# Two-layer decoder trunk with routed experts: the residual's rows turned while the experts are chosen, the last expert in two pieces, and a branch hint

## The chip, the cores and the metric

The kernel runs on one core of a Trainium2 chip. The metric is the device time of one execution in microseconds (us); the time quoted for a kernel is the median of its runs. One execution more was taken with the hardware profiler; the profile's times count from the start of that execution's span. PE is TensorE, with PEld its weight loads; ACT is ScalarE, DVE is VectorE, POOL is GpSimd, and SP is the engine whose queue carries the weight transfers.

## What is computed

A trunk of two layers over 256 tokens of width 1024, in float32. Layer 0 mixes with retention, layer 1 with native sparse attention. After each mixing comes the same end, on which the change works (cut from the reference):

```python
def moe(h, router_w, router_b, w_gate, w_up, w_down):      # 16 experts of width 512
    aff = jax.nn.sigmoid((x @ router_w).astype(jnp.float32))
    ...                                                     # best group of 4, its top 2 experts
    for e in range(N_EXPERTS):
        he = (jax.nn.silu(x @ w_gate[e]) * (x @ w_up[e])) @ w_down[e]
        y = y + w[:, e:e + 1] * he

h = layer_norm(ALPHA * h + mix, ln_mix_g[l], ln_mix_b[l])
h = layer_norm(ALPHA * h + moe(h, ...), ln_ffn_g[l], ln_ffn_b[l])
```

So each layer needs, besides the experts' outputs, the residual ALPHA * h added to them, where h is the normalised row times a per-column scale plus a shift.

## The kernel before

The 256 tokens are two blocks of 128 rows (`tb`). Every weight streams once from HBM in chunks of 1 MB over SP's queue, through a ring of SBUF places; a chunk is asked for when the place that it takes is free. Products that need float32 accuracy on f32r data use a high and a low part (`hilo`: ACT casts the high part, DVE subtracts to get the low one). The weights of the dense layers are split so as well, 1024 columns at a time (L114 on ACT, L115 on DVE); the experts' weights are multiplied as plain f32, each such matmul standing in the trace as two records.

After the mixing, `mix_norm` ends the layer's first half. It copies the rows to SBUF as `r`, transposes `r` in f32 on PE to get the router's logits, normalises `r` in place (without scale and shift), and splits it into `hh` (ACT, L569) and `hl` (POOL, L577). Then PE has to wait for DVE, which ranks the experts; in that time it is kept at work by matmuls whose results nobody reads: `warm` (L252, 20 in layer 0 and 12 in layer 1, from the table `WARM`), and two f32 matmuls of 512 columns behind it (L625). `ACT` loads its Silu table there. `route` (L681 to L683, then the one-hot matrices L709) ends the choice.

`experts` gathers each expert's tokens into 64 slots by multiplying `hh` and `hl` with one-hot matrices (L727). ACT (L735) and DVE (L733) take the result out of PSUM and apply scale and shift on the way. For each expert e the loop then runs `gate_up` of expert e+1 (16 chunk halves, L776, 64 slots by 512 columns), `hidden` (Silu on ACT L795, product on DVE L796), and `down` of expert e (L776 on hT). In the middle of a `gate_up` PE does the `fill`: `turn` (transposes of the hidden rows, L804), `scatter` (the expert's output, split by `hilo` on ACT L222 and DVE L223, is added to the four PSUM banks `y` through the one-hot matrix, L825), parts of the next gather, and the residual: `alpha` (L832 to L846). In the fills of experts 0 to 7 `alpha` transposes one 128-column part of `hh` and of `hl` for both blocks (four transposes, L837), ACT and DVE scale, shift and add them into `al` (L839, L840), and the next fill adds `al` to `y` with the matrix ALPHA * identity (L844).

The last expert has no `gate_up` beside it. So PE runs, one behind the other: down(14), turn, scatter(14), down(15), and scatter(15), which waits for ACT and DVE to split the output of down(15). Then the row statistics of the final norm start on DVE (L306).

Each expert takes 64 tokens. Should one have more, `overflow` (L862 on) does the rest in a loop under `If(most > 64)`, L880, between hidden(14) and down(13). With these inputs no expert has more, so all engines jump over that body, some hundred PE instructions. In layer 0 the splitting of the next layer's dense weights begins during the last two experts (`split_ahead`): two halves of 1024 columns before down(14), two before down(15).

Of the kernel before, what the change touches and what calls it, by code (L numbers as in the profile page):

```python
# [10 lines left out]
F32 = mybir.dt.float32  # L11
# [18 lines left out]
WARM = 10, 20, 20, 12  # L30
# [123 lines left out]
class Trunk:  # L154
# [50 lines left out]

    def split_ahead(self, n):

        self.W.limit = 2 * self.moe_end(0) + n
        self.W.ahead()
# [314 lines left out]
    def mix_norm(self, keep, pool, y, tail, hh, low_parts, l, acc):  # L524
# [23 lines left out]

        def logits(tb, nh):
# [55 lines left out]
        turn(1, 1)  # L605
        end1 = dev(1)
# [4 lines left out]
        logits(1, 1)  # L611
        minus(1)
# [20 lines left out]
        return self.sums(acc, f"y_moe{l}"), oh, rest, hl  # L633
# [80 lines left out]
    def experts(self, pool, keep, oh0, rest, hh, hl, y, l):  # L714
        nc = self.nc
        iota = self.cst[:, C_IOTA:C_IOTA + 64]
# [90 lines left out]
        def down(e, hT):  # L807

            b = [self.bank(), self.bank()]
            for k in range(4):  # L810
                both(hT[:, k, :], self.W.get(2)[0], b, k == 0, k == 3)
            if not out:
                out.append(self.first.tile([P, 2048], F32R, tag="raw", name=f"out{l}"))
            d = []
            for i in range(2):
                t = out[0][:, i * 512:i * 512 + 512]
                hi, lo = t[64 * i:64 * i + 64], t[64 - 64 * i:128 - 64 * i]
                self.hilo(hi, lo, b[i][64 * i:64 * i + 64, :])
                d.append(t)
            return d  # L820

        def scatter(e, d, last):

            o = oT[e // 4][:, e % 2, e % 4 // 2]
            return [lambda tb=tb, nh=nh: nc.tensor.matmul(y[tb][nh], o[:, tb, :], d[nh], start=(e == 0), stop=last)  # L825
                    for nh in range(2) for tb in range(2)]

        def alpha():

            ts = {}  # L830

            def scaled(k):  # L832
                c = slice(k * P, k * P + P)
                b = self.bank()
                for i, x in enumerate((hh, hl)):
                    for tb in range(2):
                        nc.tensor.transpose(b[:, (2 * i + tb) * P:(2 * i + tb + 1) * P], x[tb][:, c].bitcast(F32), self.ident)  # L837
# [736 lines left out]
```

## Time and profile before

| what | value |
|---|---|
| median of 3 runs | 890.33 us (889.71 to 890.62) |
| profiled execution: its time, its span | 891.96 us, 890.1 us |
| mean granted TensorE clock, of full speed | 0.98 |
| PE, DVE, ACT, POOL busy in the span | 95%, 46%, 38%, 6% |
| HBM, mean over the span | 291 GB/s |
| experts of layer 0, first gather to the final statistics | 228.3 to 458.0 us |
| experts of layer 1 | 647.3 to 877.1 us |

A duration of an instruction in the rows below is the time from its start to its end; matmuls overlap, so the time that one of a row of matmuls takes from PE is the distance to the next one's start. The part in brackets behind a row is the time that the engine was idle before it, and what released it.

### The profile page before, as it was taken

What the parts mean: (1) busy time and instruction counts of PE and PEld (TensorE: products, weight loads), DVE (VectorE), ACT (ScalarE), POOL (GpSimd) and SP (SyncE); (2) the same over time, 40 slices, a digit from 0 to 9 for tenths busy, and PEclk for the clock granted to TensorE, in tenths of its full rate; (3) what the DMA queues carried; (4) which work ended last, traced back from release to release, by engine and by line L of the source; (5) the groups of instructions that cost most, each with busy time, mean ns of one, the idle gap of its engine ahead of it and who ended that gap; (6) DMA issues with size and microseconds to landing.
All of it is one profiled execution on the core that took longest, in us unless ns stands there. A gap on an engine that the chain in (4) does not pass through costs nothing. (4 is left out here: it accounts for less than half of the span.)

```text
span 890.1 us, 12109 instructions
## 1 busy us (share of the span) xinstructions
PE 846.9 (95%) x4738; PEld 535.0 (60%) x4738; DVE 405.6 (46%) x817; ACT 339.7 (38%) x657; POOL 50.0 (6%) x70
## 2 busy tenths in 40 slices
PE   7999999998999999999879998999999999999993
PEld 5998989886545454453338786666744545445431
DVE  4666776864422132221077877775433222222215
ACT  4335344434332331322164455785523233232312
POOL 1000000000200000000000004220110000000001
PEclk8999999999999999999999999899999999999997
DMA  9966354578699999999943456205779999999801
GB/s 332 426 248 231 119 218 142 190 279 350 224 409 410 426 423 427 422 425 423 365 156 138 169 230 237 96 1 203 308 280 388 425 427 424 427 426 427 375 3 47
DMA packets 37283, 259.83 MB, mean 292 GB/s; under 512 B 4217, under 2 KB 4401, under 8 KB 6369
## 3 DMA queue, kind: packets, MB, share of 16 engines
q1 hardware_dynamic: 36432, 255.87, 71.3%
q0 software_dynamic: 640, 2.97, 1.0%
q8 instruction: 42, 0.69, 0.3%
q14 instruction: 25, 0.20, 0.1%
q10 hardware_dynamic: 144, 0.11, 0.0%
HBM read 257.88 MB, written 1.05 MB: 291 GB/s over the span
## 5 line engine op out<-in xcount | busy, mean ns | idle before, releaser
L776 PE MATMUL bank<-raw,xT 128*64 128x512 f32 x1024 | 233.9, 596 | 0.8 <-ACT xT L735 0.8
L776 PEld LDWEIGHTS bank<-raw,xT 128*64 128x64 f32 x1024 | 76.7, 137 | 125.9 <-issue 118.5
L115 DVE TENSOR_TENSOR st<-raw,st 128x1024 fp32r<-128x1024 f32 x92 | 111.4, 1234 | 55.4 <-ACT st L114 55.3
L114 ACT CAST st<-raw 128x1024 fp32r<-128x1024 f32 x92 | 94.5, 1048 | 80.4 <-PE bank L339 32.4
L776 PE MATMUL bank<-raw,hT 128*64 128x512 f32 x512 | 118.6, 601 | 5.2 <-PEq L880 3.3
L323 PE MATMUL bank<-xh,st 128*128 128x256 f32 x512 | 93.6, 284 | 3.0 <-ACT st L114 2.5
L223 DVE TENSOR_TENSOR out<-bank,out 64x512 fp32r<-64x512 f32 x64 | 44.1, 689 | 96.7 <-ACT out L222 95.6
L776 PEld LDWEIGHTS bank<-raw,hT 128*64 128x64 f32 x512 | 40.5, 138 | 73.3 <-issue 70.1
L323 PEld LDWEIGHTS bank<-xh,st 128*128 128x128 f32 x512 | 80.4, 192 | 3.6 <-ACT st L114 2.7
L222 ACT CAST out<-bank 64x512 fp32r<-64x512 f32 x64 | 37.1, 579 | 104.6 <-PE bank L776 103.8
L323 PE MATMUL bank<-xl,st 128*128 128x256 f32 x256 | 72.3, 283 | 0.0
L796 DVE SCALAR_TENSOR_TENSOR sh<-bank,wsl,sh 64x512 f32<-64x512 f32 x32 | 23.7, 741 | 105.3 <-ACT sh L795 105.1
L795 ACT ACTIVATE sh<-bank 64x512 f32<-64x512 f32 x32 | 19.0, 593 | 94.9 <-PE bank L776 94.9
L323 PEld LDWEIGHTS bank<-xl,st 128*128 128x128 f32 x256 | 49.6, 194 | 0.1
L805 ACT COPY hT<-bank 128x256 f32<-128x256 f32 x32 | 11.9, 373 | 86.9 <-PE bank L804 86.9
L356 PE MATMUL acc<-st,gh 128*128 128x512 f32 x128 | 42.9, 407 | 1.8 <-DVE st L115 1.1
L339 PE MATMUL bank<-st,hTh 128*128 128x512 f32 x128 | 42.2, 401 | 1.7 <-DVE nt L1022 1.4
L825 PE MATMUL y_moe<-out 128*128 128x512 f32 x128 | 38.6, 419 | 4.4 <-DVE out L223 4.4
L840 DVE SCALAR_TENSOR_TENSOR al<-bank,wsm,al 128x256 f32<-128x256 f32 x16 | 7.7, 484 | 72.0 <-ACT al L839 72.0
L339 PE MATMUL bank<-st,xh 128*128 128x512 f32 x128 | 40.5, 393 | 0.0
L733 DVE TENSOR_SCALAR xT<-bank,wsm 128x128 f32<-128x128 f32 x64 | 21.9, 404 | 34.0 <-PE bank L727 24.2
L735 ACT ACTIVATE xT<-bank,wsm 128x128 f32<-128x128 f32 x64 | 24.1, 456 | 19.3 <-PE bank L727 19.3
(328 smaller groups left out, 1205.4 us busy)
## 6 DMA issues: line engine op xcount, KB each, us to landing
raw<-in_w_moe_dram SPq DMA_DIRECT2D x190, 1024.0 KB, 10.3
raw<-in_w_dense_dram SPq DMA_DIRECT2D x49, 1024.0 KB, 7.0
raw<-in_w_moe_dram SPq DMA_DIRECT2D x4, 512.0 KB, 15.6
xT<-in_x_T_dram SPq DMA_DIRECT2D x4, 256.0 KB, 5.4
raw<-in_w_dense_dram SPq DMA_DIRECT2D x2, 512.0 KB, 10.0
rt<-in_c_ret_dram POOLq DMA_DIRECT2D x1, 1024.0 KB, 11.1
gb<-in_ln_rows_dram POOLq DMA_DIRECT2D x1, 1024.0 KB, 6.9
out_dram<-lf_n SPq DMA_DIRECT2D x4, 256.0 KB, 2.0
```

The source lines that it names most:

```text
L114: self.nc.scalar.copy(hi, r)
L115: (eng or self.nc.vector).tensor_sub(lo, r, hi.bitcast(F32))
L222: self.nc.scalar.copy(hi, src)
L223: self.nc.vector.tensor_sub(lo, src, hi.bitcast(F32))
L323: self.nc.tensor.matmul(b[:, m, :], w[:, kk, c], x[:, k, :], start=(k == 0 and i == 0 and m == 0), stop=(k == 7 and i == 2 and m == 1))
L339: self.nc.tensor.matmul(b[tb], x[:, k, c], w[:, kk, :], start=(k == 0 and i == 0), stop=(k == 7 and i == 2))
L356: self.nc.tensor.matmul(y[tb][nh], x[a][:, c], w[b][:, 0, n], start=False, stop=last and i == 2)
L733: nc.vector.tensor_scalar(t, v, c, d, op0=ALU.mult, op1=ALU.add)
L735: nc.scalar.activation(t, v, AF.Identity, bias=d, scale=c)
L776: nc.tensor.matmul(b[i][c, :], x, w[:, i, :], start=first, stop=last)
L796: nc.vector.scalar_tensor_tensor(rows[0:64], b[0:64], w, rows[0:64], op0=ALU.mult, op1=ALU.mult)
L825: return [lambda tb=tb, nh=nh: nc.tensor.matmul(y[tb][nh], o[:, tb, :], d[nh], start=(e == 0), stop=last) for nh in range(2) for tb in ran ...
```

## The change

1. **Residual.** `mix_norm` transposes the normalised f32 rows `r` themselves, eight 128-column parts for each of the two blocks (`turned`): block 0 into two banks of the rotating PSUM pool, ahead of the warm-up, block 1 into two of the banks of `y`, behind the warm-up. In `experts`, ACT alone scales and shifts them into SBUF: block 0 ahead of the first gather's evacuations, block 1 behind the issue of gate_up(0). All adds to `y` come in two lots, in the fills of gate_up(0) and gate_up(1), and now open the accumulation.
2. **Warm-up.** `WARM` goes from 20 and 12 to 8 and 8, and the two f32 matmuls of L625 go. The load of ACT's Silu table moves behind the first gather.
3. **Branch.** The If's branch gets a hint "likely taken" for PE, placed at the start of the block in which the If stands.
4. **Dense weights.** In layer 0 three halves are split right behind the If, ahead of the splitting of down(13)'s output; the fourth follows later, in the final norm.
5. **Last expert.** The transposes for expert 15 stand in the middle of down(14); down(15) runs as two pieces of 256 columns, each with its own splitting by ACT and DVE; scatter(14) stands behind the second piece.

The core of the diff:

```diff
-WARM = 10, 20, 20, 12
+WARM = 10, 20, 8, 8
@@ mix_norm
+        def turned(tb, nh, b):
+            for k in range(4):
+                nc.tensor.transpose(b[:, k * P:k * P + P], half(r, tb, nh)[:, k * P:k * P + P], self.ident)
...
         turn(1, 1)
+        y_moe = self.sums(acc, f"y_moe{l}")
+        rows = [[self.bank() for _ in range(2)], y_moe[1]]
+        turned(0, 0, rows[0][0])
...
         logits(1, 1)
+        turned(0, 1, rows[0][1])
...
-        self.ready(AF.Silu)
         self.warm(self.bits, WARM[2 + l])
-        b = self.bank()
-        for _ in range(2):
-            nc.tensor.matmul(b, r[1][:, 0:P], r[1][:, left], start=True, stop=True)
+        for nh in range(2):
+            turned(1, nh, rows[1][nh])
@@ experts
-        def down(e, hT):
+        def down(hT, t, parts=1, fill=()):
...
+            n = 512 // parts
+            for p in range(parts):
+                c = slice(p * n, p * n + n)
+                for k in range(4):
+                    if k == 2 and p == 0:
+                        for f in fill:
+                            f()
+                    if p == 0:
+                        ws.append(self.W.take(2)[0] if k and parts > 1 else self.W.get(2)[0])
+                    both(hT[:, k, :], ws[k][:, :, c], [v[:, c] for v in b], k == 0, k == 3)
+                for i in range(2):
+                    v = t[:, i * 512 + c.start:i * 512 + c.stop]
+                    self.hilo(v[64 * i:64 * i + 64], v[64 - 64 * i:128 - 64 * i], b[i][64 * i:64 * i + 64, c])
...
+        def alpha(tb, t):
+            def scaled():
+                for k in range(8):
+                    v, c, d = turned[tb][k // 4][:, k % 4 * P:k % 4 * P + P], sc[:, k:k + 1], sh[:, k:k + 1]
+                    nc.scalar.activation(t[:, k, :], v, AF.Identity, bias=d, scale=c)
+            def add():
+                for k in range(8):
+                    nc.tensor.matmul(y[tb][k // 4][:, k % 4 * P:k % 4 * P + P], t[:, k, :], self.ai, start=(k % 4 == 0), stop=False)
+            return scaled, add
@@ overflow
+            self.tc.mark_branch_hint_location(f"past{l}", "LikelyTaken", engines=(mybir.EngineType.PE,))
-            with self.tc.If(most > 64), self.tc.For_i(0, NE, 1) as e:
+            with self.tc.If(most > 64, label=f"past{l}"), self.tc.For_i(0, NE, 1) as e:
@@ the loop over experts
+        scale[0]()
         first, second = gather(0)
+        self.ready(AF.Silu)
-        b = gate_up(0, [first, second, rest], 1)
+        b = gate_up(0, [first, second, rest, adds[0]], 1)
+        scale[1]()
...
             if e == 13:
                 overflow()
-            if l == 0 and e >= NE - 2:
-                self.split_ahead(2 * (e - NE + 3))
-            d = down(e, hT)
+                if l == 0:
+                    self.W.limit = 2 * self.moe_end(0) + 3
+                    self.W.ahead()
...
+                between.append(lambda: turn(last))
+            d = down(hT, out[0], 1, between)
...
+        d_last = down(last, spare(F32R, "d_last"), 2)
+        for f in scatter(NE - 2, d, False):
+            f()
         self.ready(AF.Sqrt)
-        for f in scatter(NE - 1, d, True):
+        for f in scatter(NE - 1, d_last, True):
```

How PE's instructions stand at the end of `mix_norm` in layer 0, before (L545 is `turn`, L553 the logits, L252 the warm-up, whose 20 pairs are cut to one, L681 the ranking, L727 the gather):

```order
L545 MATMUL bank_2085<-cst,r_1963 128x128 x4
L553 MATMUL bank_2069<-wp_832,rT_2090 128x16 x4
L252 LDWEIGHTS bits
L252 MATMUL bank_2123<-bits 128x384
...
L625 MATMUL bank_2144<-r_1963 128x512 x2
L681 LDWEIGHTS bits
L681 MATMUL bank_2177<-ch_2170,bits 128x16
...
L727 MATMUL bank_2198<-oh_0_2183,hh_1957 128x256 x2
```

And after (line numbers are the changed file's: L540 is `turn`, L547 is `turned`, L247 the warm-up, of which 8 pairs are left, L683 the ranking):

```order
L540 MATMUL bank_2085<-cst,r_1963 128x128 x4
L547 MATMUL bank_2096<-cst,r_1962 128x128 x4
L553 MATMUL bank_2069<-wp_832,rT_2090 128x16 x4
L547 MATMUL bank_2097<-cst,r_1962 128x128 x4
L247 LDWEIGHTS bits
L247 MATMUL bank_2136<-bits 128x384
...
L547 MATMUL y_moe_10_2094<-cst,r_1963 128x128 x4
L547 MATMUL y_moe_11_2095<-cst,r_1963 128x128 x4
L683 LDWEIGHTS bits
L683 MATMUL bank_2183<-ch_2176,bits 128x16
```

Block 0's second four transposes stand ahead of the warm-up, and block 1's eight, into two banks of `y`, between the warm-up and the ranking, in the place of L625.

How ACT's instructions stand around the If of layer 0, before (the L795 ahead of the If is hidden(14), the one behind it hidden(15); L222 is the splitting of an expert's output, L805 the copy of the turned rows, L114 the splitting of dense weights; the If's body is cut):

```order
L795 ACTIVATE sh_2194<-bank_3334 64x512
...
L880 COMPARE_AND_BRANCH x2
...
L880 COMPARE_AND_BRANCH
L880 UNCONDITIONAL_BRANCH x2
L222 CAST out_2353<-bank_3711 64x512
L222 CAST out_2353<-bank_3712 64x512
L805 COPY hT_14_3729<-bank_3743 128x256
L795 ACTIVATE sh_2194<-bank_3730 64x512
L114 CAST st_3763<-raw_3339 128x1024
L114 CAST st_3766<-raw_3339 128x1024
L222 CAST out_2353<-bank_3769 64x512
```

And after (L799, L883, L217 and L809 are the same lines in the changed file):

```order
L799 ACTIVATE sh_2197<-bank_3290 64x512
...
L883 COMPARE_AND_BRANCH x2
...
L883 COMPARE_AND_BRANCH
L883 UNCONDITIONAL_BRANCH x2
L114 CAST st_3668<-raw_3295 128x1024
L114 CAST st_3671<-raw_3295 128x1024
L114 CAST st_3674<-raw_3311 128x1024
L217 CAST out_2369<-bank_3677 64x512
L217 CAST out_2369<-bank_3678 64x512
L809 COPY hT_14_3695<-bank_3709 128x256
L799 ACTIVATE sh_2197<-bank_3696 64x512
```

Three splittings of dense weights moved from behind hidden(15) to the first place behind the If, ahead of the two casts that down(13)'s output needs. On DVE their subtractions moved in the same way.

How PE's instructions stand at the end of layer 1's experts, before (L776 is `down`, L804 the transposes of `turn`, L825 `scatter`; of the repeated matmuls the last is shown):

```order
L776 MATMUL bank_7346<-raw_6855,hT_14_7311 64x512
L804 MATMUL bank_7360<-cst,sh_5762 128x128 x4
L825 MATMUL y_moe_00_5752<-out_5925 128x512
...
L825 MATMUL y_moe_11_5755<-out_5925 128x512
L776 MATMUL bank_7370<-raw_6861,hT_15_7359 64x512
...
L776 MATMUL bank_7371<-raw_6892,hT_15_7359 64x512
L825 MATMUL y_moe_00_5752<-out_5925 128x512
```

And after (L780, L808 and L834 are these lines):

```order
L780 MATMUL bank_7282<-raw_6777,hT_14_7246 64x512
L808 MATMUL bank_7287<-cst,sh_5743 128x128 x4
L780 MATMUL bank_7281<-raw_6789,hT_14_7246 64x512
...
L780 MATMUL bank_7282<-raw_6789,hT_14_7246 64x512
L780 MATMUL bank_7302<-raw_6795,hT_last_7280 64x256
...
L780 MATMUL bank_7303<-raw_6826,hT_last_7280 64x256
L780 MATMUL bank_7302<-raw_6795,hT_last_7280 64x256
...
L780 MATMUL bank_7303<-raw_6826,hT_last_7280 64x256
L834 MATMUL y_moe_00_5637<-out_5917 128x512
...
L834 MATMUL y_moe_11_5640<-out_5917 128x512
L834 MATMUL y_moe_00_5637<-d_last_7301,out_5917 128x512
```

The transposes moved up into the middle of down(14), down(15) became two runs over 256 columns of the same chunks, and scatter(14) moved from ahead of down(15) to behind its second piece.

## Rows read from the trace of the kernel before

**Rows 1.** Stretches: busy us (instructions) of PE, PEld, DVE, ACT, POOL; granted clock; DMA share, GB/s
```profile
244.00:430.00 186.00, 184.05 (x978) 86.68 (x973) 42.86 (x81) 51.39 (x102) 0.00 (x0) 1.00 1.01 421
551.00:554.40 3.40, 1.12 (x8) 0.67 (x6) 3.23 (x8) 1.54 (x8) 3.32 (x4) 1.00 0.65 270
554.40:559.00 4.60, 3.87 (x16) 2.60 (x17) 4.57 (x10) 3.01 (x11) 4.45 (x6) 0.50 0.00 0
431.30:436.30 5.00, 4.89 (x13) 1.71 (x14) 0.00 (x0) 0.00 (x0) 0.83 (x2) 0.66 0.78 288
850.00:857.00 7.00, 5.27 (x26) 2.13 (x26) 1.52 (x3) 1.75 (x3) 0.00 (x0) 1.00 0.02 6
```

**Rows 2.** Timeline of PE behind the If, layer 0: start us, us, instructions [idle before]
```profile
431.33 4.89 PE L776 MATMUL bank<-raw,hT 128*64 128x512 f32 x13 [3.27 <-PEq L880]
```

**Rows 3.** Timeline of PE, layer 1, the last two experts
```profile
865.00 3.60 PE L776 MATMUL bank<-raw,hT 128*64 128x512 f32 x16
...
869.99 1.46 PE L825 MATMUL y_moe<-out 128*128 128x512 f32 x4 [0.80 <-DVE out L223]
871.37 3.65 PE L776 MATMUL bank<-raw,hT 128*64 128x512 f32 x16
876.41 1.46 PE L825 MATMUL y_moe<-out 128*128 128x512 f32 x4 [1.38 <-DVE out L223]
```

**Rows 4.** Timeline of PE, one fill in layer 1
```profile
678.10 0.38 PE L837 MATMUL bank<-cst,hh 128*128 128x128 f32 x2
...
678.46 0.48 PE L727 MATMUL bank<-oh,hh 128*128 128x256 f32 x2
```

**Rows 5.** Timeline of ACT, layer 0, the end of mix_norm and first gather
```profile
223.62 1.50 ACT L618 ACTIVATE r<-r,mr,mx_y 128x512 f32<-128x512 f32 x2
...
230.83 1.50 ACT L735 ACTIVATE xT<-bank,wsm 128x128 f32<-128x128 f32 x4 [3.16 <-PE bank L727]
```

**Rows 6.** Timeline of PE in the same stretch
```profile
222.34 3.41 PE L252 MATMUL bank<-bits 128*128 128x384 bf16 x20
...
227.30 0.17 PE L681 MATMUL bank<-ch,bits 128*128 128x16 bf16 x1
...
228.27 0.50 PE L727 MATMUL bank<-oh,hh 128*128 128x256 f32 x2 [0.74 <-DVE oh L709]
```

**Rows 7.** Timeline of PEld: the weight load ahead of the first ranking matmul
```profile
226.97 0.10 PEld L681 LDWEIGHTS <-bits 128*128 128x128 bf16 x1 [0.34 <-DVE ch L677]
```

**Rows 8.** Timeline of PE, layer 1, the first ranking matmul
```profile
646.14 0.18 PE L681 MATMUL bank<-ch,bits 128*128 128x16 bf16 x1 [0.51 <-DVE ch L677]
```

**Rows 9.** The If's line L880: ns min/median/max, first and last start
```profile
L880 PEldq COMPARE_BRANCH  x2: 3632/4760/5888, 425.0 to 847.0; - x2
...
L880 DVEq COMPARE_BRANCH  x2: 62/67/72, 429.4 to 851.3; - x2
L880 DVEq EVENT_SEMAPHORE  x2: 21/21/21, 430.0 to 851.7; - x2
```

**Rows 10.** SP's queue: the two dense chunks that are split first
```profile
421.28 2.04 SPq L92 DMA_DIRECT2D raw<-in_w_dense_dram  x2
```

**Rows 11.** The page's DMA issues: KB each, median us from issue to landing
```profile
raw<-in_w_moe_dram SPq DMA_DIRECT2D x190, 1024.0 KB, 10.3
raw<-in_w_dense_dram SPq DMA_DIRECT2D x49, 1024.0 KB, 7.0
```

**Rows 12.** The page's groups: busy us, mean ns of one | idle before, its releaser
```profile
L115 DVE TENSOR_TENSOR st<-raw,st 128x1024 fp32r<-128x1024 f32 x92 | 111.4, 1234 | 55.4 <-ACT st L114 55.3
L114 ACT CAST st<-raw 128x1024 fp32r<-128x1024 f32 x92 | 94.5, 1048 | 80.4 <-PE bank L339 32.4
...
L776 PEld LDWEIGHTS bank<-raw,hT 128*64 128x64 f32 x512 | 40.5, 138 | 73.3 <-issue 70.1
```

**Rows 13.** Timeline of DVE, layer 1, the end of the experts
```profile
875.67 1.41 DVE L223 TENSOR_TENSOR out<-bank,out 64x512 fp32r<-64x512 f32 x2 [5.01 <-ACT out L222]
877.11 1.89 DVE L306 BATCH_NORM_STATS2 lf_st<-y_moe 128x6 f32<-128x512 f32 x3
```

More of the change, by code (lines that the diff above doesn't have):

```diff
@@ L805, in turn @@
             nc.scalar.copy(hT, b.rearrange("p (k s) -> p k s", k=4)[:, :, 0:64])
-        def down(e, hT):
+        def down(hT, t, parts=1, fill=()):
             b = [self.bank(), self.bank()]
[L810 to L820, printed above, removed]
+            ws = []
+            n = 512 // parts
[11 more added lines that the diff above has]
+                    self.hilo(v[64 * i:64 * i + 64], v[64 - 64 * i:128 - 64 * i], b[i][64 * i:64 * i + 64, c])
+            return [t[:, i * 512:i * 512 + 512] for i in range(2)]
@@ L822, in scatter @@
         def scatter(e, d, last):
             o = oT[e // 4][:, e % 2, e % 4 // 2]
[L825 removed]
+            return [lambda tb=tb, nh=nh: nc.tensor.matmul(y[tb][nh], o[:, tb, :], d[nh], start=False, stop=last)
                     for nh in range(2) for tb in range(2)]
[L828 to L837, printed above, removed]
[L838 to L846 removed]
@@ L925, in experts @@
             nc.gpsimd.dma_start(piece, self.t["ln_rows"][3].rearrange("a (p n) -> p a n", p=8))
+        scale, adds = zip(*(alpha(tb, scaled_rows) for tb in range(2)))
+        scale[0]()
         first, second = gather(0)
-        b = gate_up(0, [first, second, rest], 1)
+        self.ready(AF.Silu)
+        b = gate_up(0, [first, second, rest, adds[0]], 1)
+        scale[1]()
         weigh(0)
@@ L930, in experts @@
         d = self.gb = None
-        picks, todo, more = [], [], alpha()
-        for e in range(NE):
+        picks, todo = [], []
+        spare = lambda dtype, name: pool.tile([P, 1024], dtype, tag="xT", name=f"{name}{l}", bufs=3)
+        for e in range(NE - 1):
             g = e // 4 + 1
@@ L941, in experts @@
             if e + 1 < NE:
-                fill += more[:1] + picks[:2] + todo[:2]
-                more, picks, todo = more[1:], picks[2:], todo[2:]
-                b = gate_up(e + 1, fill)
-                if e % 4 == 2 and g < 4:
-                    weigh(g)
-                hidden(e + 1, b)
-            else:
-                for f in fill:
-                    f()
+                fill += ([] if e else [adds[1]]) + picks[:2] + todo[:2]
+            picks, todo = picks[2:], todo[2:]
+            b = gate_up(e + 1, fill)
+            if e % 4 == 2 and g < 4:
+                weigh(g)
+            hidden(e + 1, b)
             if e == 13:
                 overflow()
-            if l == 0 and e >= NE - 2:
-                self.split_ahead(2 * (e - NE + 3))
-            d = down(e, hT)
+                if l == 0:
+                    self.W.limit = 2 * self.moe_end(0) + 3
+                    self.W.ahead()
+            if e == 0:
+                out.append(self.first.tile([P, 2048], F32R, tag="raw", name=f"out{l}"))
+            between = []
+            if e == NE - 2:
+                last = spare(F32, "hT_last")[:, 0:256].rearrange("p (k s) -> p k s", k=4)
+                between.append(lambda: turn(last))
+            d = down(hT, out[0], 1, between)
             if e == 0:
@@ L985, in ffn @@
             with self.phase(f"exp{l}") as ep:
-                self.experts(ep, pool, oh, rest, hh, hl, y, l)
+                self.experts(ep, pool, oh, rest, hh, hl, y, l, turned)
                 if l == 1:
```

17 lines of the change are left out of this document (4 added, 13 removed).

## The prediction

> **What bounds the kernel now.** I read the stretches first. From 244 to 430 us PE is busy 184.05 of 186.00 us, while the DMA engines are full as well (share 1.01, 421 GB/s) [rows 1]. So in the experts a PE instruction taken out is time won, as long as the weights stay ahead. They do: the two chunks for the next layer, which follow layer 0's last expert chunk in the same queue, are issued from 421.28 us on [rows 10], so the last expert chunk was asked for before that and landed at the latest with them, by about 432; PE begins down(15) 5.7 us before the statistics (871.37 against 877.11 in layer 1 [rows 3, 13]), in layer 0 at 452.3. The lead is some 20 us. What is left to win are PE's holes. I looked for them in PE's timeline: 3.27 us behind the If in layer 0, with the clock low behind it [rows 2], and 0.80 and 1.38 us in the last two experts, both ended by DVE [rows 3]. The third place is the wait for the ranking ahead of the first gather.
>
> **Residual.** In the fills of experts 0 to 7 the four transposes of `alpha` hold PE from 678.10 to 678.46 us [rows 4], 0.36 us; eight fills make 2.9 us per layer, all on the path, since PE has no holes there. The adds stay as many (16 matmuls per layer, merely in two lots), so they count nothing. The DVE and ACT steps of `alpha` go, but those engines waited for PE anyway. What comes in: 16 transposes per layer ahead of the ranking (priced with the warm-up) and 16 ACT activations of 128 columns. Four such take 1.50 us [rows 5], so a block takes 3.0 us. Block 0's stand ahead of the gather's evacuations: ACT is free 3.16 us before the first of these, at 227.67 [rows 5], and now even 1.5 us earlier, since the table load has moved. They fit: 0. Block 1's stand beside gate_up(0), which lasts longer than 3.0 us; 0 again. If either cover failed, up to 3.0 us per layer would come back.
>
> **Warm-up.** In layer 0 the ranking's weights could be loaded at 226.97, when DVE was done [rows 7], but PE came to the matmul only at 227.30 [rows 6]: the warm-up was too long by 0.33 us, and this goes. In layer 1 PE already waited 0.51 us there [rows 8]; 0. The risk is the clock. Twenty warm-up matmuls take 3.41 us from 222.34 on [rows 6], 0.17 each; eight, behind four of the new transposes, end at about 224.2. Then come eight transposes, 0.09 each, held up by ACT's normalising until 225.12 [rows 5], the ranking at 227.0 and the gather, 0.97 us after that as before [rows 6], at 227.9. In these 3.7 us PE is busy for about 1.0, 27%, where before it had one hole of 0.74. The trace has a stretch of nearly that kind: 551.0 to 554.4, 1.12 of 3.40 us busy, and behind it the clock was 0.50 [rows 1], which is the lower of the two levels, 1.2 GHz. From 850.0 to 857.0, with one hole of 1.73 us, it stayed at 1.00 [rows 1]. The new stretch is nearer to the first, so I take a fall in both layers. Its price: behind the If 13 records took 4.89 us at a mean clock of 0.66 [rows 1, 2]; at 3.65 us for 16 [rows 3] they take 2.97, so one fall costs 1.9 us of dense work. In the gather PE also waits for ACT and DVE, which hides a part: 0 to 1.9, I take 1.0 per layer.
>
> The Trainium skill (TensorE: Matmul & The Clock Gate, Part 4) says that transposes do not count as busy for the clock in the way that matmuls do; no row here shows transposes by themselves. By that page the new stretch is emptier than I counted, and with the full price of 1.9 in both layers the time would be 879.7.
>
> **Branch hint.** PE's sequencer spends 5.89 us (the maximum) and 3.63 us (the minimum) in the If's taken branch, DVE's 0.07 [rows 9]. In layer 0 that ends PE's hole at 431.33 [rows 2]. With the branch free, PE still has to meet the other engines behind the If: DVE passes at 430.0 [rows 9], after hidden(14). So at most 431.33 - 430.0 - 0.2 for the signal = 1.1 us go, and what is late next is hidden(14). In layer 1 DVE passes only at 851.7 [rows 9], and PE's branch, from 847.0 on, was over at 850.63: 0. The hole of layer 0 shrinks from 3.27 to some 2.15 us, between full work on both sides. That is nearer to the 1.73 us of layer 1, behind which the clock stayed full [rows 1], than to 3.27, behind which it fell; so I take the 1.9 us of the fall as saved too, bounds 0 and 1.9.
>
> The Trainium skill (Runtime: NRT & Kernel Launch, Instruction fetch mechanics) states that a taken branch to code outside the loaded window waits for a fetch; the 5.89 us agree. It knows of no hint; by the page as it stands nothing would be won here, which is the second rival's 880.9.
>
> **Dense weights.** Three casts on ACT (1.048 us each) and three subtractions on DVE (1.234) [rows 12] now stand ahead of the splitting of down(13)'s output, and they wait for chunks issued from 421.28 to about 423 [rows 10]. Nothing makes these land earlier: the queue is full [rows 1]. With 7.0 us to land as for dense chunks, or 10.3 as for the experts' [rows 11], they land at 428.3 and 430.0, or at 431.6 and 433.3. DVE then ends the three at 433.0 or 436.3, and the output's first half, 0.7 later [rows 13], is there at 433.7 or 437.0. Who waits is scatter(13) on PE: PE leaves the If at 427.9 (430.2 less 2.2 won so far), runs down(13) and half of gate_up(15), 3.65 each, and the transposes, and comes to it at 435.7. So 0 to 2.0 us are lost; between the ends I take 0.3. Who gains from the splittings' leaving their old places is nobody on the path. The fourth goes into the final norm, where ACT and DVE have slack: 0, or 1.2 if not.
>
> **Last expert.** Before, from down(14) at 865.00 [rows 3] to the statistics at 877.11 [rows 13] are 12.1 us. After: down(14) with the transposes, 869.99 - 0.80 - 865.00 = 4.2 us [rows 3]; both pieces of down(15), if half the columns take half the time, 3.65 together; then scatter(14) covers the splitting of piece 2. On DVE that is two times 0.44, by 0.70 for 512 [rows 13] and 1.234 for 1024 columns [rows 12], behind an ACT cast of some 0.35: DVE is done at 4.2 + 3.65 + 1.2 = 9.1 us, PE with scatter(14) and the first matmuls of scatter(15) at 9.1 to 9.6. I take 9.3: 2.8 us won per layer. The pieces need twice the weight loads, 0.138 each [rows 12]; should these, and not the columns, set the pace, 32 of them make 4.4 us and 0.8 of the gain goes.
>
> **The sum.** Layer 0: -2.9 - 0.33 + 1.0 - 1.1 - 1.9 + 0.3 - 2.8 = -7.7. Layer 1: -2.9 + 1.0 - 2.8 = -4.7. Together -12.4: the profiled execution of 891.96 becomes 879.5, and the median of 890.33, which lies 1.6 below it, 877.9.
>
> **The rivals.** (1) The clock does not fall in the routing stages: 2.0 less, of which some 0.4 comes back because PE then reaches scatter(13) earlier: 876.3. For it speaks that in before such stretches as 850 to 857 kept it. (2) The hint does nothing: the hole of 3.27 and the fall behind it stay, the wait for the dense chunks disappears in them: +1.1 + 1.9 - 0.3, 880.6 to 880.9. (3) The hint works, but the clock falls all the same: 879.5 to 879.8. (4) The dense chunks land as the experts' do: +1.7, 879.6; or PE, faster by 2.9 us, catches up with the weights in layer 0: 880.8; the lead of some 20 us speaks against that. (5) The moved steps do not leave the path: ACT's activations hold up the gather and hidden(0), 3.0 us for each of four blocks, and the gain shrinks to nearly nothing: 889.9. Against it stands ACT's idle time in rows 5. (6) Slower: at its place, the stretch ahead of the gather, the clock falls and does not come back while PE works through the experts. Each us at 1.2 GHz costs half a us of dense work; from 25 us of it on, both layers together, the gain of 12.4 is gone, and with 50 us the time is 890.3 + 12.6 = 902.9. Against it: the low stretches behind the holes end after 5 us [rows 1, 2].
>
> **How the numbers follow.** The forecast, 877 to 879: 0.37. Rivals: (1) 0.17, (2) 0.13, (3) 0.17, (4) 0.08, (5) 0.05, (6) 0.03. The range takes in rivals 1 to 4 with their bounds: below, no clock loss in the routing (2.0), no wait for the dense chunks (0.3), 3.0 instead of 2.8 for each tail and 0.7 for the spread of runs, 874.5; above, the hint without effect, both falls at 1.9 and weight loads that set the pace of the pieces, 884. About 0.2%, 1.8 us, is what can be told from no change: faster 0.94, same 0.03 (a part of 5), slower 0.03.
>
> **What would show it.** In the fills no four transposes ahead of the gather's steps; PE's hole behind layer 0's If at 2.2 us or less, ended by DVE, with clock 1.00 behind it; from down(14) to the statistics 9.3 us in both layers; clock below 1.00 from 228 to 233 and in the same stage of layer 1; scatter(13) of layer 0 waiting at most 0.4 us for DVE. A PE wait ended by ACT's activations at the gather, or by a chunk, would make the prediction wrong, and so would low clock for over 6 us.

## The result and the profile after

| | before | after |
|---|---|---|
| median | 890.48 us (889.71 to 891.28, 4 runs) | 881.88 us (878.86 to 884.19, 4 runs) |
| ratio after/before, 95% interval | | 0.9897 (0.9875 to 0.9919) |
| profiled execution, its span | 891.96, 890.1 us | 884.19, 882.4 us |

The kernel is faster by 1.0%, about 9 us; 12.4 were forecast. The time lies in the range, some 4 us above the point of 877.9.

To see where it went I cut the span at three places of each layer that can be read from the timelines: the first gather matmul, the start of down(14), and the start of the final statistics on DVE. All of these are starts of rows such as those in [rows 3, 6, 13].

| stage (us) | before | after | moved | forecast |
|---|---|---|---|---|
| start to first gather, layer 0 | 228.27 | 228.80 | +0.5 | -0.3 |
| layer 0, first gather to down(14) | 217.58 | 214.63 | -2.9 | -4.6 |
| layer 0, down(14) to statistics | 12.11 | 10.76 | -1.35 | -2.8 |
| next rows, attention, choice of layer 1 | 189.38 | 189.12 | -0.3 | 0 |
| layer 1, first gather to down(14) | 217.66 | 215.29 | -2.4 | -1.9 |
| layer 1, down(14) to statistics | 12.11 | 10.77 | -1.34 | -2.8 |
| last norm | 12.99 | 13.03 | 0.0 | 0 |

The clock in three stretches of the profile after (columns as in [rows 1]): the first gather of layer 0, the work behind its If, and the first gather of layer 1.

```profile
228.80:233.80 5.00, 4.71 (x22) 3.01 (x24) 2.10 (x5) 2.92 (x7) 2.55 (x4) 0.67 0.03 7
428.37:433.37 5.00, 5.00 (x16) 1.94 (x18) 0.00 (x0) 0.26 (x1) 0.90 (x2) 0.66 1.03 427
643.30:648.30 5.00, 4.87 (x22) 3.83 (x24) 1.84 (x5) 2.23 (x7) 3.15 (x5) 0.66 0.17 70
```

All three lay below full speed, the first and third as forecast, the second against the forecast. What stood ahead of the first, in PE's timeline (to be held against [rows 6]):

```profile
224.99 1.36 PE L547 MATMUL y_moe<-cst,r 128*128 128x128 f32 x8 [0.21 <-ACT r L622]
227.49 0.17 PE L683 MATMUL bank<-ch,bits 128*128 128x16 bf16 x1 [1.14 <-DVE ch L679]
...
228.80 0.47 PE L731 MATMUL bank<-oh,hh 128*128 128x256 f32 x2 [1.09 <-DVE oh L711]
```

The same engine behind layer 0's If, the counterpart of [rows 2]:

```profile
428.37 5.35 PE L780 MATMUL bank<-raw,hT 128*64 128x512 f32 x16 [2.16 <-DVEq L883]
433.52 3.63 PE L780 MATMUL bank<-raw,xT 128*64 128x512 f32 x16
437.09 0.66 PE L808 MATMUL bank<-cst,sh 128*128 128x128 f32 x4
438.56 1.46 PE L834 MATMUL y_moe<-out 128*128 128x512 f32 x4 [0.81 <-DVE out L218]
```

The hole is 2.16 us instead of 3.27 and DVE ends it, as forecast. But down(13) took 5.35 us, 1.7 more than its 3.65 at full clock, and scatter(13) waited 0.81 us for DVE. ACT's timeline shows why:

```profile
433.11 1.99 ACT L114 CAST st<-raw 128x1024 fp32r<-128x1024 f32 x2 [6.25 <-DMA raw<-in_w_dense_dram]
435.48 1.04 ACT L114 CAST st<-raw 128x1024 fp32r<-128x1024 f32 x1 [0.38 <-DMA raw<-in_w_dense_dram]
436.55 1.18 ACT L217 CAST out<-bank 64x512 fp32r<-64x512 f32 x2
```

The casts stood in front of down(13)'s output and waited for a chunk until 433.1 us. Last, the end of layer 1's experts on PE (counterpart of [rows 3]) and on DVE (of [rows 13]):

```profile
858.60 1.89 PE L780 MATMUL bank<-raw,hT 128*64 128x512 f32 x8
860.41 0.65 PE L808 MATMUL bank<-cst,sh 128*128 128x128 f32 x4
861.00 1.94 PE L780 MATMUL bank<-raw,hT 128*64 128x512 f32 x8
862.77 1.90 PE L780 MATMUL bank<-raw,hT_last 128*64 128x256 f32 x16
865.56 2.40 PE L780 MATMUL bank<-raw,hT_last 128*64 128x256 f32 x16 [0.90 <-DVE d_last L218]
867.89 1.21 PE L834 MATMUL y_moe<-out 128*128 128x512 f32 x4
868.94 1.09 PE L834 MATMUL y_moe<-d_last,out 128*128 128x512 f32 x4
```

```profile
867.98 0.88 DVE L218 TENSOR_TENSOR d_last<-bank,d_last 64x256 fp32r<-64x256 f32 x2 [2.02 <-ACT d_last L217]
869.37 1.30 DVE L301 BATCH_NORM_STATS2 lf_st<-y_moe 128x6 f32<-128x512 f32 x2 [0.52 <-PE y_moe L834]
```

The second piece waits 0.90 us for DVE, which is splitting the first: the splitting that should have run beside the second piece runs ahead of it. So three losses had to be explained: the clock, the dense chunks, and the tail.

### The profile page after: what moved, and what is told of

It reads as the page before. It is cut to its first block, busy times and chain, and to the rows that moved or that the text cites. A ratio compares the mean times of both kernels' runs of the same rounds, so it can differ in the third digit from the quotient of the medians.

```text
span 882.4 us, 12089 instructions
## 1 busy us (share of the span) xinstructions
PE 841.2 (95%) x4714; PEld 533.0 (60%) x4714; DVE 398.8 (45%) x805; ACT 343.1 (39%) x677; POOL 50.0 (6%) x70
## 5 line engine op out<-in xcount | busy, mean ns | idle before, releaser
L780 PE MATMUL bank<-raw,xT 128*64 128x512 f32 x1024 | 234.4, 598 | 0.2
L780 PEld LDWEIGHTS bank<-raw,xT 128*64 128x64 f32 x1024 | 76.8, 137 | 127.1 <-issue 118.8
L114 ACT CAST st<-raw 128x1024 fp32r<-128x1024 f32 x92 | 94.7, 1048 | 85.4 <-PE bank L334 29.0
L780 PE MATMUL bank<-raw,hT 128*64 128x512 f32 x480 | 111.1, 602 | 4.0 <-DVEq L883 4.0
L218 DVE TENSOR_TENSOR out<-bank,out 64x512 fp32r<-64x512 f32 x60 | 41.3, 689 | 85.5 <-ACT out L217 84.6
L780 PEld LDWEIGHTS bank<-raw,hT 128*64 128x64 f32 x480 | 38.0, 138 | 66.7 <-issue 64.0
L217 ACT CAST out<-bank 64x512 fp32r<-64x512 f32 x60 | 34.8, 580 | 87.7 <-PE bank L780 87.0
L799 ACT ACTIVATE sh<-bank 64x512 f32<-64x512 f32 x32 | 19.0, 594 | 101.0 <-PE bank L780 101.0
L809 ACT COPY hT<-bank 128x256 f32<-128x256 f32 x30 | 11.2, 373 | 83.5 <-PE bank L808 83.4
L834 PE MATMUL y_moe<-out 128*128 128x512 f32 x120 | 35.5, 416 | 0.8 <-DVE out L218 0.8
L351 PEld LDWEIGHTS acc<-st,gh 128*128 128x128 f32 x128 | 24.5, 193 | 8.6 <-DVE st L115 2.2
```

Of the source, the lines that this page charges most:

```text
L114: self.nc.scalar.copy(hi, r)
L217: self.nc.scalar.copy(hi, src)
L218: self.nc.vector.tensor_sub(lo, src, hi.bitcast(F32))
L351: self.nc.tensor.matmul(y[tb][nh], x[a][:, c], w[b][:, 0, n], start=False, stop=last and i == 2)
L780: nc.tensor.matmul(b[i][c, :], x, w[:, i, :], start=first, stop=last)
```

## The experiments

Each run gives a median and one profile. The stage from layer 0's statistics to layer 1's first gather, with the attention, took 186.0 to 189.4 us over the profiles; the granted clock from 540 to 560 and from 560 to 580 us was 0.86 and 0.88 in before, 0.91 and 1.00 in e4_nohint. Where this blurs the median, the stage times decide. They come from one execution of each version. "After" is the changed kernel. Each ratio is to the kernel before, run on the same chip.

**Other banks for the second piece.**

```diff
-            b = [self.bank(), self.bank()]
             for p in range(parts):
+                b = [self.bank(), self.bank()]
```

> The changed kernel, but the second piece of down(15) writes two other PSUM banks than the first. Theory: in the changed kernel the second piece waits 0.90 us because it writes the banks that DVE still reads; with other banks only the splitting of down(14)'s output can hold it, which ends 0.3 us after piece 1. The wait falls from 0.90 to about 0.3 us, the distance from down(14) to the final statistics from 10.8 to 10.1-10.2 us in both layers, the median by 1.2 us. Rival: short pieces cost PE more by themselves (the second took 2.33 us, the first 1.85): then the second takes 2.3 us in other banks too and the distance stays above 10.5 us.

Measured: ratio 0.9873 (0.9843 to 0.9904). From down(14) to the statistics 9.78 us in both layers. PE's timeline, layer 0:

```profile
448.72 4.21 PE L780 MATMUL bank<-raw,hT_last 128*64 128x256 f32 x32
452.86 1.20 PE L834 MATMUL y_moe<-out 128*128 128x512 f32 x4
```

The wait is gone altogether, where 0.3 us of it was expected to stay: the two pieces now are one run of 32 records. The theory holds: the shared banks were the cause. What the rival said is there too, but small: 32 records take 4.14 us, where 16 of twice the width take 3.53 in the next run.

**One piece again.**

```diff
-        d_last = down(last, spare(F32R, "d_last"), 2)
+        d_last = down(last, spare(F32R, "d_last"), 1)
```

> The changed kernel with down(15) in one piece again (the transposes for expert 15 still inside down(14), scatter(14) still behind down(15)). Theory: in the changed kernel the two pieces bring nothing, since the second waits 0.90 us for DVE; the gain of 1.35 us comes from the moved transposes and scatter(14). In one piece the splitting of 512 columns (about 2.0 us) lies bare behind down(15) but for scatter(14)'s 1.1 us: from down(14) to the statistics 10.3 to 10.8 us in layer 1, no worse than the 10.77 of the two pieces. Rival: the two pieces save about half of that splitting even so: 11.5 us.

Measured: ratio 0.9903 (0.9874 to 0.9933). From down(14) to the statistics 9.85 and 9.86 us, 0.9 better than the two pieces of after. In layer 1:

```profile
865.16 3.60 PE L780 MATMUL bank<-raw,hT_last 128*64 128x512 f32 x16
868.69 1.20 PE L834 MATMUL y_moe<-out 128*128 128x512 f32 x4
870.15 1.46 PE L834 MATMUL y_moe<-d_last,out 128*128 128x512 f32 x4 [0.26 <-DVE d_last L218]
```

scatter(14), moved behind down(15), already hides the splitting but for 0.26 us. One piece takes 3.53 us where the two took 4.14 in the run above. So the whole gain of the tail, 2.25 us, comes from the moved transposes and the moved scatter(14). The pieces as built cost 0.9, and in banks of their own they bring 0.08. The expected 10.3 to 10.8 us was missed by the step that scatter(14) covers only 1.1 us of the splitting; that the pieces bring nothing was right. In layer 0 this execution also showed the largest wait for the dense chunks:

```profile
439.60 2.08 PE L834 MATMUL y_moe<-out 128*128 128x512 f32 x4 [4.81 <-DVE out L218]
441.60 5.80 PE L780 MATMUL bank<-raw,xT 128*64 128x512 f32 x16
```

4.81 us, and a clock of 0.50 behind it (5.80 us for 16 records). Layer 0 took 218.41 us to down(14) there, more than before the change, although the clock was 1.00 at its first gather and behind its If.

**Dense splittings one expert later** (from behind the If to ahead of down(14)).

```diff
             if e == 13:
                 overflow()
+            if e == 14:
                 if l == 0:
                     self.W.limit = 2 * self.moe_end(0) + 3
```

> The changed kernel, but layer 0's three splittings of dense weights stand ahead of down(14) instead of right behind the If. Theory: behind the If they made ACT and DVE wait for chunks that landed 13.6 us after their issue, and scatter(13) waited 0.81 us for it; one expert later the chunks have landed, the wait of 0.81 us is gone and nothing else comes late: the median falls by 0.5 to 0.8 us. Rival: there they hold up the copy of expert 15's transposed rows and the splitting of down(14)'s output, and a wait of as much appears at down(15): no change.

Measured: ratio 0.9878 (0.9854 to 0.9901). scatter(13) no longer waits; first gather to down(14) 213.32 us, 1.3 less than after, with the clock low in the same two places. From there to the statistics 11.01 instead of 10.76: a part of the rival, 0.25 us.

**Six warm-up matmuls ahead of the ranking.**

```diff
         for nh in range(2):
             turned(1, nh, rows[1][nh])
+        self.warm(self.bits, 6)
```

> The changed kernel with six more warm-up matmuls behind block 1's transposes, in PE's wait of 1.14 us for the ranking. Theory: the clock fell at the first gather (0.77 in layer 0, 0.56 in layer 1) because PE was mostly idle ahead of it; with the hole filled it stays at 1.00 in both layers, the stretch from the first gather matmul to the last add of block 0 shrinks by 0.9 us in layer 0 and 1.4 us in layer 1, the median by about 2 us. Rival: what counts is that transposes and short matmuls stand there, or the second hole of 1.1 us behind the ranking: the clock falls as before and the time stays within 0.5 us.

Measured: ratio 0.9891 (0.986 to 0.9921). The clock was 1.00 in both first gathers, and layer 1 took 214.23 us to down(14), 1.06 less than after. Layer 0 won nothing, 215.15 us against 214.63. Its PE arrived early and met the dense chunks:

```profile
437.31 1.46 PE L835 MATMUL y_moe<-out 128*128 128x512 f32 x4 [2.63 <-DVE out L218]
438.70 5.35 PE L781 MATMUL bank<-raw,xT 128*64 128x512 f32 x16
```

It was at full clock behind the If, but the wait grew from 0.81 to 2.63 us, and behind this wait the clock fell instead (5.35 for 16 records). So in layer 0 the moved splittings take back what PE gains ahead of them.

**Residual adds one expert later** (block 0 in the fill of gate_up(1), block 1 in gate_up(2)).

```diff
-        b = gate_up(0, [first, second, rest, adds[0]], 1)
-        scale[1]()
+        b = gate_up(0, [first, second, rest], 1)
...
+            fill = [lambda: turn(hT)] + ([adds[e]] if e < 2 else []) + (scatter(e - 1, d, False) if e else [])
...
             b = gate_up(e + 1, fill)
+            if e == 0:
+                scale[1]()
```

> The changed kernel with the two lots of residual adds one expert later (block 0 in the fill of gate_up(1), block 1 in that of gate_up(2)). Theory: in the changed kernel block 0's lot, 2.0 us of PE in the middle of the first gate_up, together with the low clock there, keeps the first weight places occupied longer, so the weight stream, which is full from then on to 430 us, runs 4 us later than before and the dense chunks land at 433 instead of 429 us; with the adds later the first places come free 2 us earlier, the dense chunks land 1.5 to 2 us earlier against the first gather, and scatter(13)'s wait of 0.8 us is gone: from the first gather to down(14) 213.8 us in layer 0; layer 1 within 0.2 us of the changed kernel. Rival: the stream's start is set by something else (the low clock alone, or the places that the new tiles take): landing and wait as in the changed kernel.

Measured: ratio 0.9902 (0.9873 to 0.993); layer 0 to down(14) 212.03 us; layer 1 214.13. ACT's first dense cast starts 201.7 us after the first gather, against 204.3 in after; before, the chunks landed after some 200.8. The whole kernel's busy times and DMA rate from 226 to 250 us, for before, after and this one in that order:

```profile
226.00:250.00 24.00, 22.57 (x133) 11.90 (x133) 7.38 (x27) 6.44 (x15) 3.92 (x6) 1.00 0.64 238
```

```profile
226.00:250.00 24.00, 21.48 (x135) 13.36 (x132) 7.66 (x29) 11.68 (x30) 3.85 (x6) 0.93 0.51 197
```

```profile
226.00:250.00 24.00, 21.28 (x134) 12.33 (x134) 7.39 (x27) 11.40 (x29) 3.84 (x6) 1.00 0.65 252
```

In after the stream lost 41 GB/s over 24 us, 1.0 MB or 2.3 us of a full queue. From 250 to 300 us it lost another 11 GB/s, 1.3 us, and from 300 us on the rates are alike (424 to 426). Together that is 3.6 us; counted from the first gather, the chunks land 3.5 later. With the later adds the loss is gone up to 250 us, but not behind it:

```profile
250.00:300.00 50.00, 50.00 (x276) 24.46 (x272) 13.50 (x26) 14.88 (x30) 0.00 (x0) 1.00 1.00 411
```

```profile
250.00:300.00 50.00, 50.00 (x267) 23.13 (x267) 10.72 (x22) 12.95 (x27) 0.00 (x0) 1.00 1.00 400
```

```profile
250.00:300.00 50.00, 50.00 (x270) 23.81 (x268) 12.04 (x23) 13.45 (x27) 0.00 (x0) 1.00 0.97 393
```

Two other executions tell the adds from the clock, since they had the adds in their old place and the clock at 1.00 at the first gather (e2_fill and e8_one, in that order):

```profile
226.00:250.00 24.00, 22.28 (x150) 14.04 (x150) 7.57 (x28) 11.61 (x30) 3.83 (x6) 1.00 0.56 207
```

```profile
226.00:250.00 24.00, 21.30 (x143) 13.62 (x143) 7.69 (x30) 11.70 (x30) 3.84 (x6) 1.00 0.57 216
```

| execution | adds | clock at the first gather | GB/s, 226 to 250 and 250 to 300 us | first dense cast behind the first gather, us |
|---|---|---|---|---|
| after, e1_banks, e4_nohint | early | 0.66 to 0.68 | 190 to 202, 396 to 400 | 204.3, 205.4, 205.2 |
| e2_fill, e8_one | early | 1.00 | 207, 216; 409, 397 | 203.1, 204.0 |
| e7_later | later | 1.00 | 252, 393 | 201.7 |

So at the same full clock the early adds (with block 1's scaling on ACT, which the edit moves too) cost 1.4 to 2.3 us of landing, and the low clock 0.3 to 2.3 on top, in executions that differ by 1.1 among themselves. The rival, that the low clock alone sets the stream's start, falls. The forecast of no wait failed: PE came earlier as well, and waited 1.31 us. Nor are the 2.6 us by which layer 0 is shorter than in after the work of the later adds: 1.7 of them is down(13) at full clock (3.65 instead of 5.35 us), and the first gather too ran at 1.00.

**No hint.** The marking line is taken out of after.

> The changed kernel without the branch hint. Theory: the hint took 1.1 us out of layer 0's hole behind the If (3.27 to 2.16 us) but not the fall of the clock behind it, and nothing in layer 1; without it the hole is 3.2 us again, scatter(13) no longer waits 0.81 us for DVE because PE comes later, so the median rises by only 0.3 us. Rival: the hint is worth its 1.1 us in full: the median rises by 1.1 us; or it does nothing and the hole was shortened by the other changes: no change and a hole of 2.2 us.

Measured: ratio 0.9893 (0.9873 to 0.9913). The hole is 3.33 us in layer 0 and 2.33 in layer 1, both ended by PE's sequencer. Layer 0 to down(14) 215.51 us (after 214.63), layer 1 214.67 against 214.23 where the clock was 1.00 with the hint. So in after the hint is worth about 0.9 and 0.4 us, with no wait for the dense chunks in layer 0 without it. The medians can't show this: that of the run without the hint is even lower (880.12 against 881.88), well inside the spread of either. PE's branch itself, without the hint here and with it in after (ns):

```profile
L882 PEldq COMPARE_BRANCH  x2: 5128/5535/5942, 421.9 to 835.9; - x2
```

```profile
L883 PEldq COMPARE_BRANCH  x2: 388/1686/2984, 423.2 to 840.4; - x2
```

With the hint it is short in layer 0 (0.39 us) but not in layer 1 of after, where it still took 2.98 us; there it was over before DVE passed, and the hole of 1.89 us is ended by DVE.

**The hint alone, on the kernel before.**

```diff
+            self.tc.mark_branch_hint_location(f"past{l}", "LikelyTaken", engines=(mybir.EngineType.PE,))
             most = nc.values_load(self.cnt[0:1, 0:1], min_val=0, max_val=2 * P)
-            with self.tc.If(most > 64), self.tc.For_i(0, NE, 1) as e:
+            with self.tc.If(most > 64, label=f"past{l}"), self.tc.For_i(0, NE, 1) as e:
```

> The kernel before with the branch hint alone. Theory: the hint takes PE's branch off the hole behind the If of layer 0: 3.27 becomes 2.2 us, ended by DVE, while the clock falls behind it as before (0.66); from the first gather to down(14) 216.5 instead of 217.6 us; in layer 1, where DVE ended the hole before too, 0. Median 1.1 us less. Rival: with the shorter hole the clock stays: 214.6 us, median 2.9 less. Or the hint does nothing in this code: 217.6.

Measured: 886.0 us, ratio 0.9949 (0.9931 to 0.9966), 3.0 to 6.1 us less. PE behind the If, and the branch instruction itself (ns):

```profile
430.87 3.65 PE L776 MATMUL bank<-raw,hT 128*64 128x512 f32 x16 [2.18 <-DVEq L881]
```

```profile
L881 PEldq COMPARE_BRANCH  x2: 350/372/393, 425.7 to 841.3; - x2
```

The branch took 0.35 to 0.39 us instead of 3.63 and 5.89 [rows 9]; the hole shrank to 2.18, and behind it the clock was full. Layer 0 to down(14) 213.95 us, 3.6 less; layer 1 217.65, 0.0. The rival came true: behind the shorter hole the clock did not fall in this execution. That the median of the ten runs is lower by at least 3.0 us, where the shorter hole alone gives 1.1, fits this.

**Filling the If's hole** (eleven warm-up matmuls ahead of the If; dense splittings one expert later as above).

```diff
             if e == 13:
+                self.warm(self.bits, 11)
                 overflow()
```

> The changed kernel with the dense splittings one expert later (as in the run e3_split14) and, besides, eleven warm-up matmuls on PE ahead of the If, in its hole of 2.16 us. Theory: the hole lets the clock fall behind the If, and with the hole filled down(13) runs in 3.65 instead of 5.35 us; since no splitting of dense weights stands ahead of down(13)'s output, this gain reaches the end: from the first gather to down(14) 211.6 us in layer 0, against 213.3 without the warm-up matmuls and 214.6 in the changed kernel; median 1.7 us below e3_split14. Rival 1: the clock falls whatever PE does there: 213.3. Rival 2: the warm-up matmuls make the branch or the next matmul later than the hole lasts: above 213.5.

Measured: ratio 0.9879 (0.9848 to 0.9911). PE there:

```profile
424.12 1.96 PE L247 MATMUL bank<-bits 128*128 128x384 bf16 x11
426.58 3.65 PE L780 MATMUL bank<-raw,hT 128*64 128x512 f32 x16 [0.50 <-PEq L883]
```

down(13) ran in 3.65 us and nothing waited. Layer 0 to down(14) took 212.46 us, not 211.6: in this execution the clock at the first gathers was 0.50, lower than in e3_split14, and layer 1 took 216.64. The part at the If is as expected.

**All four corrections** (banks, both lots of warm-up matmuls, later splittings), the same with one piece, and the first once more with more rounds.

> The changed kernel with four corrections: other PSUM banks for the second piece, six warm-up matmuls ahead of the ranking, eleven ahead of the If, and the dense splittings one expert later. Theory: the four losses found are separate and all add up: layer 0 from the first gather to down(14) 210.6 us (214.6 in the changed kernel), from there to the statistics 10.0 (10.8), layer 1 214.2 (215.3) and 9.8 (10.8); in all 6.9 us less than the changed kernel, median about 875 us, ratio to the kernel before 0.983. Rival: they take each other's gain, since the weight stream sets layer 0's pace: layer 0 stays above 212.5, median 877 or more.

> The kernel of e10_all with down(15) in one piece, for the choice between one piece and two pieces in separate banks. Theory: two pieces in separate banks hide half of the splitting, one piece none of it: from down(14) to the statistics 10.4 us in layer 1 against 9.8, the median 1.2 us above e12_all_again. Rival: equal within 0.3 us per layer, since scatter(14) hides it either way.

> The kernel of e10_all once more, beside e11_all_one and with more rounds, for its interval: ratio to the kernel before 0.984 to 0.987; the clock at 1.00 at both first gathers and behind layer 0's If, as in e10_all. Rival: the falls come and go by chance whatever stands in the holes: one of these three stretches is below 0.8 in this execution.

| run | median, ratio (interval) | layer 0: to down(14), to statistics | layer 1 | clock: gather 0, If, gather 1 |
|---|---|---|---|---|
| e10_all | 877.86, 0.9857 (0.983 to 0.9883) | 210.55, 10.11 | 214.65, 9.78 | 1.00, 1.00, 1.00 |
| e11_all_one | 876.87, 0.9841 (0.9813 to 0.9869) | 211.77, 9.86 | 214.65, 9.85 | 0.66, 1.00, 1.00 |
| e12_all_again | 875.77, 0.9836 (0.9807 to 0.9865) | 211.84, 10.11 | 214.63, 9.78 | 0.66, 1.00, 1.00 |

In e10_all, where the clock fell in none of the three places, the losses are separate and add up: 210.55 us was expected as 210.6. Its median is 2.9 us above the expected 875, and in the other two executions, with a fall at the first gather, layer 0 took 1.2 and 1.3 us more. One piece or two in separate banks is the same within 0.25 us per layer, so of e11_all_one's two answers the second holds. Layer 1 kept 0.4 us more than expected, since eleven warm-up matmuls make PE reach the branch 0.41 us too late there. The version is faster than the kernel before in all three runs. Against after (0.9875 to 0.9919) the intervals of e11_all_one and e12_all_again lie below, that of e10_all overlaps it. But e11 and e12 show the rival of the last expectation at the first gather: the clock fell there in spite of the filling.

**The clock over all profiles.** The first gather of layer 0 was below full speed in 5 of 7 executions with the short warm-up (after, e1, e3, e4, e6; not e7, e8), of layer 1 in 4 of 7 (after, e1, e6, e8). With six warm-up matmuls more it was 2 of 4 and 0 of 4; with the old warm-up (before and e9) 0 of 2 and 0 of 2. A fall cost 1.0 to 1.3 us (1.06 in layer 1 between after and e2; 1.29 in layer 0 between e12 and e10), with a clock of 0.50 about 2. Behind layer 0's If the clock fell in 2 of 2 executions with a hole of 3.3 us, in 3 of 7 with 2.2 us, and in 0 of 4 with the hole filled. With 2.2 us it fell in just those executions in which it had fallen at the first gather. Behind scatter(13)'s wait for the dense chunks it stayed at full speed after 0.81, 1.31 and 1.92 us (after, e7, e1: 3.65 us for the next 16 records) and fell after 2.63 and 4.81 (e2, e8: 5.35 and 5.80). What decides it within one and the same code I could not settle.

## Why the prediction was right, and where it was off

The direction held, and the residual, the fall of the clock at the first gathers and the hole at the branch went as described. Three steps failed: the clock behind the If, the landing of the dense chunks, and the overlap of the last expert's two pieces. The time lies in the range because the range had room for most of this, and also because the residual won 1.4 us more than forecast, which was luck. By its number the second rival (880.9, the hint does nothing) lies nearest, but it is not what happened.

For the first step, a fill of layer 1 before the change, and the two lots of adds in e3_split14, each with the start of what follows:

```profile
708.07 0.61 PE L844 MATMUL y_moe<-ai,al 128*128 128x128 f32 x4
708.51 0.38 PE L837 MATMUL bank<-cst,hh 128*128 128x128 f32 x2
708.73 0.38 PE L837 MATMUL bank<-cst,hl 128*128 128x128 f32 x2
709.04 3.65 PE L776 MATMUL bank<-raw,xT 128*64 128x512 f32 x16
```

```profile
646.43 2.03 PE L847 MATMUL y_moe<-ai,al 128*128 128x128 f32 x16
648.39 5.37 PE L780 MATMUL bank<-raw,xT 128*64 128x512 f32 x24
658.55 1.95 PE L847 MATMUL y_moe<-ai,al 128*128 128x128 f32 x16
660.43 1.94 PE L780 MATMUL bank<-raw,xT 128*64 128x512 f32 x8
```

The steps:

- **Residual: right, but mis-sized.** Forecast 2.9 us per layer. In layer 1 at full clock (e3_split14) the stage is 3.4 shorter although its hole behind the If is 0.16 longer, so 3.6. From `turn` to `turn` seven fills are 0.88 us shorter each (15.66 to 14.78 us in one of them), and the one from which only the last add goes 0.43 (12.84 to 12.41). So the transposes were worth 0.45 us per fill, not 0.36, and 3.7 in the layer. (In the fill shown they hold PE for 0.53 us, but without them the step from the scatter to the next matmul is 0.08 longer.) The forecast's 0.36 ends in [rows 4] at the start of the gather's first matmuls, and the step from these to the next ones was longer behind the transposes, 0.31 us against 0.23. The adds, which the forecast put at nothing, became dearer: two lots of 1.96 and 1.88 us against eight times some 0.44, 0.3 to 0.4 more. Some 0.2 us came off the first gather. ACT's scaling stayed hidden, as costed.
- **Warm-up: the clock term right, the 0.33 us wrong.** PE met the ranking 0.19 us later, not earlier: the stages ahead ran 0.5 late in this execution, so that DVE's input to the ranking came late by as much. From the ranking's matmul to the gather it took 1.31 instead of 0.97 us. The first of DVE's two one-hot instructions ends that chain; it took 0.68 us instead of 0.43. Why, no run shows; in layer 1 of the kernel before it took 0.65 as well. The fall came in both layers and cost 1.06 in layer 1, for 1.0 taken. That it comes in only some executions was not in the forecast.
- **Branch: hole right, clock mis-sized.** 3.27 became 2.16 us, ended by DVE. The step that failed is "I take the 1.9 us of the fall as saved too": in after it was not, in the kernel before with the hint it was. The third rival describes this step of after. That layer 1 would gain nothing was right for the kernel before (e9: 0.0), not for after, where 0.4 us hang on it: without the hint the branch took 5.13 us there, 1.5 more than before, and so PE's own branch ended the hole. The Trainium skill (Runtime: NRT & Kernel Launch, Instruction fetch mechanics) has a taken branch wait for a fetch when its target lies outside the loaded window. The long branches without the hint, 5.1 and 5.9 us in e4_nohint, fit that; whether the target lay outside, and what the hint does about it, no run shows.
- **Dense chunks: the term that failed in kind.** Forecast 0.3 us with landing 7.0 to 10.3 us after the issue. They were issued 1.84 us earlier (419.44 against [rows 10]) and landed 13.9 us after it (median of the two; before 7.8), the first at 433.1. "Nothing makes these land earlier" was right; that the change makes them land later was missed. The early lots of adds, and the low clock on top, made the stream lose bytes up to 300 us (e7_later and the table there), and a queue that is full until 430 us carries this delay to its end. The wait was 0.81 us in after, and 0 to 4.81 over the executions with the splittings in that place. The forecast's own upper end is a slip besides: 437.0 less 435.7 is 1.3 us, not 2.0, since scatter(13) starts on the output's first half (in after DVE's splitting starts at 437.82, and PE goes on at 438.56).
- **Last expert: the step "both pieces, 3.65 together; then scatter(14) covers the splitting of piece 2" failed.** Forecast 9.3, measured 10.77: 0.90 of wait for the shared banks, and 0.5 to 0.6 for 16 more records with their weight loads, which the text held possible with 0.8. The order listing showed both pieces writing the same banks; I read the columns as apart and did not ask for waits between them.

Against 12.4: tails 2.9 less, clock behind the If 1.9 less (it fell before and after), dense wait 0.5 less, start and warm-up 0.9 less, residual 1.4 more. That makes 7.6; the spans differ by 7.7.

## What to carry to other kernels

Work moved ahead on a queue that waits for a transfer makes everything behind it wait for that transfer; where the weight stream is full, ask what holds its first places longer, since the delay comes out where the stream ends. In this kernel two pieces overlapped only when the second wrote to banks that nobody was reading; and first try whether other work behind the long step, here scatter(14), hides the same thing for nothing. When PE work is taken away ahead of a wait, price the clock behind that wait from rows and from several executions, not one.

## What was not expected of the hardware

PE's taken branch over the If's body cost 3.63 to 5.94 us in four profiled instances, in two kernels without a hint. With one it cost 0.35 to 0.46 us in 17 of 22 instances, in layer 0 always; in layer 1 it still took 2.92 to 2.98 us in after, e1_banks, e3_split14 and e7_later, and 1.68 in e2_fill. Two chunks issued 1.84 us earlier into a full queue landed 4 us later (433.1 against some 429). The clock behind the same 2.16 to 2.18 us hole fell to 0.66 in three executions and stayed at 1.00 in four. In the runs of the result the changed kernel's times spread over 5.3 us, those of the kernel before over 1.6; but beside e8_one, e11_all_one and e12_all_again the kernel before spread over 5.1 us as well (889.47 to 894.56).
